# Products of the first four tiles of two modulation vectors on TensorE instead of VectorE

## The chip, the cores and the metric

The kernel runs on one core of a Trainium2 chip. The metric is device microseconds of that core for one execution; the time before is 2090.2 us, the median of 3 runs (2087.49 to 2090.66). Lower is better.

## The reference, cut to what matters

The model is two small transformer stacks, one after the other, on 256 tokens of width 1024. What the change touches is the very first step: the shift and the scale of the first normalisation, which are a matrix-vector product each.

```python
mod = (jax.nn.silu(c) @ ada_w[layer] + ada_b[layer]).reshape(B, 3, 3, D)
h = modulate_pre(x, g[0, 0], mod[:, 0, 0], mod[:, 0, 1])   # rms_norm(x, g) * (1 + scale) + shift
y = swiglu_ffn(h, ffn_w_in[layer, 0], ffn_w_out[layer, 0])
```

`c` is one row of 1024 numbers and each of shift and scale has 1024 entries, so either costs a read of a 1024 x 1024 float32 matrix (4 MB) that is used once.

## The kernel before, in words

All work is float32. Activations stand transposed, as 8 tiles `k` of 128 features x 256 tokens, and every large product is made of three products of rounded halves (`hi`, `lo`), marked fp32r in the trace. Weights come in pieces of 128 x 1024 float32 (512 KB) through one pool of six buffers, `raw`, each read by a transfer that SyncE (SP) issues as soon as a buffer is free; SP issues them in a fixed order.

`first_ffn` starts the program. It needs, for every tile `k`, two columns of 128 numbers: `b` (shift) and `a` (from the scale). Before the change both are made by VectorE (DVE): line 312 multiplies a 128 x 1024 piece of `ada_w`, laid out with outputs on partitions, by `srow`, a row silu(c) spread over all partitions, and sums along the row. Lines 315 to 317 add the bias and fold in the gain. A second chain makes the norm: `x` is loaded (line 267), turned by 16 TensorE (PE) transposes (line 274) that ScalarE (ACT) copies out (line 275), while ACT squares and sums `x` (line 395, four times), GpSimd (POOL) makes the reciprocal root of it (lines 402 to 404), PE spreads it over partitions (line 432) and ACT copies it out as `rb` (line 434). Only then can DVE make `tmp = xT * a * rb` (line 319), ACT `hi` (line 320) and DVE `lo` (line 321) of a tile.

A string sets how the eight tiles (A) and the first four weight blocks (W, each two pieces: line 300 on ACT, line 301 on DVE) follow each other in the program's text:

```python
 'start': 'AAAWAWAWAWAA',
```

`xk` is 2, so the pieces of tiles 0 and 1 are asked for ahead of `x`. `unit(s, k)` (lines 282 to 290) is the PE work of weight block `s` on tile `k`, six products of 128 x 256. A scheduler then orders each engine's instructions by its own forecast of times; the order on an engine is fixed from there on, and each engine takes its instructions in that order.

Of the kernel before, what the change touches and what calls it, by code (L numbers as in the profile page):

```python
# [13 lines left out]
F32 = mybir.dt.float32  # L14
BF16 = mybir.dt.bfloat16
F32R = mybir.dt.float32r
AF = mybir.ActivationFunctionType
ALU = mybir.AluOpType
# [3 lines left out]
P = 128  # L22
D = 1024
KT = D // P
# [61 lines left out]
class Kern:  # L86
# [176 lines left out]
    def first_ffn(self, g, win):  # L263
        nc, I = self.nc, self.I
        srow = self.srow(0)
        raws = [self.raw_half(I["ada_w"][v][k]) for k in range(self.cfg["xk"]) for v in range(2)]
        nc.sync.dma_start(self.x, I["x"])
        xT = self.chunk().rearrange("p (k t) -> p k t", k=KT)
        for q in range(4):
# [9 lines left out]
        ab = self.cp.tile([P, KT, 2], F32, name=self.name("AB"))  # L279
# [13 lines left out]
        for item in self.cfg["start"]:  # L293
            if item == "W":
                s = len(ws)
                whi, wlo = self.chunk(F32R), self.chunk(F32R)
                for half in range(2):
                    c = slice(half * 1024, (half + 1) * 1024)
                    raw = self.raw_half(win[s][:, c])
                    nc.scalar.copy(whi[:, c], raw)  # L300
                    nc.vector.tensor_tensor(wlo[:, c], raw, whi[:, c].bitcast(F32), op=ALU.subtract)
                ws.append([(whi[:, h * 1024:(h + 1) * 1024], wlo[:, h * 1024:(h + 1) * 1024]) for h in range(2)])
                pss.append([self.ps([P, T], "ps" if s < 3 else "fps") for _ in range(2)])
                for k in range(done):
                    unit(s, k)
                continue
            k = done
            a, b = ab[:, k, 1:2], ab[:, k, 0:1]
            for v in range(2):
                raw = raws[2 * k + v] if 2 * k < len(raws) else self.raw_half(I["ada_w"][v][k])  # L310
                junk = self.w([P, D], "vjunk", bufs=1, dt=BF16)
                nc.vector.scalar_tensor_tensor(junk, raw, 1.0, srow, op0=ALU.mult, op1=ALU.mult,
                                               accum_out=ab[:, k, v:v + 1])
            bb, ba = (self.col("ada_b", v * 8 + k, 1) for v in range(2))
            nc.vector.tensor_tensor(b, b, bb, op=ALU.add)
            nc.vector.tensor_scalar(a, a, ba, 1.0, op0=ALU.add, op1=ALU.add)
            nc.vector.tensor_tensor(a, a, g[:, k:k + 1], op=ALU.mult)
            tmp = self.w([P, T], "htmp", bufs=2)
            nc.vector.scalar_tensor_tensor(tmp, xT[:, k], a, rb, op0=ALU.mult, op1=ALU.mult)
            nc.scalar.activation(hi[:, k], tmp, AF.Identity, bias=b)  # L320
            nc.vector.scalar_tensor_tensor(lo[:, k], tmp, b, hi[:, k].bitcast(F32), op0=ALU.add, op1=ALU.subtract)
            done += 1
            for s in range(len(ws)):
                unit(s, k)
# [1132 lines left out]
def host_layout(a):  # L1457
    f = lambda z: np.ascontiguousarray(z)
# [16 lines left out]
    def vecs(w):  # L1475
        return w.reshape(D, -1, KT, P).transpose(1, 2, 3, 0)
# [5 lines left out]
    o = {}  # L1482
# [2 lines left out]
    o["crow"] = f(np.stack([a["c"].reshape(D), a["c_2"].reshape(D), a["c_ctx_2"].reshape(D)]))  # L1485
    o["ctx"] = toks(a["ctx_2"])
    o["ada_w"] = f(np.concatenate([vecs(a["ada_w"][l]) for l in range(2)]))
    o["kv_ada_w"] = f(vecs(a["kv_ada_w"]))
    o["ada_w2"] = f(np.concatenate([vecs(a["ada_w_2"][l]) for l in range(2)]))
    o["ffn_w_in"] = f(np.concatenate([ffin(a["ffn_w_in"][l, i]) for l in range(2) for i in range(2)] + [ffin(a["ffn_w_gu_2"][l]) for l in range(2)]))  # L1490
# [75 lines left out]
```

## Time and profile before

| what | value |
|---|---|
| runs, median (range) | 2090.2 us (2087.49 to 2090.66) |
| the profiled execution | 2091.53 us, its span 2089.8 us |
| busy share of the span: PE, DVE, ACT, POOL | 95%, 78%, 52%, 7% |
| PE busy in the first of 40 slices (0 to 52 us), and in the next ones | 5 tenths; 9 tenths or more |
| chain that ended last: PE, DVE | 68%, 14% of the span |

The span runs from the first to the last instruction; the execution's own time is 1.7 us longer. The page gives the mean over the whole program. The change works in the first 50 us, so what is read below is the trace of that stretch.

### The profile page before, as it was taken

What the parts mean: (1) busy time and instruction counts of PE and PEld (TensorE: products, weight loads), DVE (VectorE), ACT (ScalarE), POOL (GpSimd) and SP (SyncE); (2) the same over time, 40 slices, a digit from 0 to 9 for tenths busy, and PEclk for the clock granted to TensorE, in tenths of its full rate; (3) what the DMA queues carried; (4) which work ended last, traced back from release to release, by engine and by line L of the source; (5) the groups of instructions that cost most, each with busy time, mean ns of one, the idle gap of its engine ahead of it and who ended that gap; (6) DMA issues with size and microseconds to landing.
All of it is one profiled execution on the core that took longest, in us unless ns stands there. A gap on an engine that the chain in (4) does not pass through costs nothing.

```text
span 2089.8 us, 34683 instructions
## 1 busy us (share of the span) xinstructions
PE 1995.1 (95%) x13158; PEld 1783.2 (85%) x13158; DVE 1625.2 (78%) x2753; ACT 1094.3 (52%) x1775; POOL 138.6 (7%) x188
## 2 busy tenths in 40 slices
PE   5999999999999999999999999999999999999998
PEld 5998797999889878888778999878888999778997
DVE  7878898877887788789988666889879855866454
ACT  3444545444554466657655444548755444564443
POOL 0000202000100000120001000210010000100000
PEclk9999999999999999999999999999999999999999
DMA  9999787899877775576457767565456955514553
GB/s 331 326 320 341 253 321 279 323 321 316 280 243 258 255 231 181 186 255 209 166 169 251 268 232 237 190 207 190 162 176 233 348 191 193 165 61 160 185 188 114
DMA packets 136327, 486.46 MB, mean 233 GB/s; under 512 B 14976, under 2 KB 16480, under 8 KB 135392
## 3 DMA queue, kind: packets, MB, share of 16 engines
q1 hardware_dynamic: 134240, 477.90, 66.9%
q0 software_dynamic: 1728, 6.29, 0.9%
q8 instruction: 103, 1.69, 0.3%
q14 instruction: 64, 0.52, 0.1%
q10 hardware_dynamic: 192, 0.05, 0.0%
HBM read 480.47 MB, written 3.19 MB: 231 GB/s over the span
## 4 chain that ended last, share of the span: by engine, by line
PE 68%; DVE 14%; ACT 5%; DMA 5%; issue 4%; POOL 3%; SPq 0%; DVEq 0%; POOLq 0%; ACTq 0%
DMA x<-in_x 0%; DVE x L641 0%; DVE xc L649 0%; DMA raw.kv.1194_6453<-in_kv_v 0%; PE ps.a10.1298_7028 L744 0%; ACT chunk.a11.1957_10411 L870 0%; DMA raw.a11.1891_10022<-in_ada_w 0%; PE ps.a10.1253_6706 L744 0%; ACT chunk.ctx.1429_7781 L1050 0%; DMA raw.a10.1424_7749<-in_ada_w 0%; DMA raw.a12.2451_13229<-in_ada_w 0%; DMA raw.a10.1455_7896<-in_ada_w 0%; POOL rqx L387 0%; DMA raw.bffn0.3229_17294<-in_ffn_w_in 0%; DMA raw.bffn0.3136_16851<-in_ada_w 0%
## 5 line engine op out<-in xcount | busy, mean ns | idle before, releaser
L1050 ACT ACT_TABLE_LOAD x16 | 20.5, 1283 | 1.7 <-DVE dst.diff0.2922_15807 L1048 1.4
L341 ACT ACT_TABLE_LOAD x16 | 20.5, 1283 | 0.3
L274 PE MATMUL ps.a00.6_101<-ident,x 128*128 128x128 f32 x4 | 1.1, 428 | 13.9 <-DMA x<-in_x 13.9
L274 PEld LDWEIGHTS ps.a00.6_101<-ident,x 128*128 128x128 f32 x4 | 0.7, 217 | 13.9 <-issue 13.9
L376 POOL DMA_DIRECT2D G.a12.2544_13849<-row.a12.2543_13847 x1 | 0.6, 595 | 179.5 <-DMA row.a12.2543_13847<-diag.a12.2542_13845 179.5
L376 POOL DMA_DIRECT2D G.bffn2.3890_21467<-row.bffn2.3889_21465 x1 | 0.6, 595 | 172.0 <-DMA row.bffn2.3889_21465<-diag.bffn2.3888_21463 172.0
L376 POOL DMA_DIRECT2D G.a02.1038_5659<-row.a02.1037_5657 x1 | 0.6, 612 | 166.1 <-DMA row.a02.1037_5657<-diag.a02.1036_5655 166.1
L334 ACT ACT_TABLE_LOAD x9 | 11.5, 1283 | 0.2
L376 POOL DMA_DIRECT2D G.bffn0.3422_18599<-row.bffn0.3421_18597 x1 | 0.6, 595 | 164.5 <-DMA row.bffn0.3421_18597<-diag.bffn0.3420_18595 164.5
L402 POOL TENSOR_TENSOR rv.ctx.354_2048<-ss.ctx.352_2044,epsd 128x1 f32<-128x1 f32 x1 | 0.2, 189 | 169.8 <-ACT junk.ctx.351_2043 L395 169.8
L376 POOL DMA_DIRECT2D G.a11.2178_11711<-row.a11.2177_11709 x1 | 0.6, 595 | 156.5 <-DMA row.a11.2177_11709<-diag.a11.2176_11707 156.5
L734 ACT ACTIVATE chunk.a10.1248_6656<-chunk.kv.1130_6083,cols 128x60 f32<-128x60 f32 x32 | 10.3, 385 | 0.8 <-ACT chunk.kv.1220_6568 L461 0.8
L288 PE MATMUL ps.a00.38_198<-chunk.a00.20_148,chunk.a00.34_188 128*128 128x256 f32 x8 | 3.2, 405 | 5.4 <-ACT chunk.a00.34_188 L300 2.9
L485 ACT CAST chunk.a01.490_2583<-chunk.a01.492_2585 128x256 fp32r<-128x256 f32 x8 | 3.2, 406 | 9.1 <-DVE chunk.a01.492_2585 L677 9.1
L288 PEld LDWEIGHTS ps.a00.38_198<-chunk.a00.20_148,chunk.a00.34_188 128*128 128x128 f32 x8 | 1.9, 236 | 6.4 <-ACT chunk.a00.20_148 L320 3.2
L387 POOL TENSOR_TENSOR rqc<-rv.ctx.1311_7159,nhalf 128x8 f32<-128x8 f32 x1 | 1.6, 1647 | 80.5 <-DVE rv.ctx.1311_7159 L383 80.5
L870 ACT ACT_TABLE_LOAD x5 | 6.4, 1283 | 0.1
L976 DVE TENSOR_TENSOR chunk.diff0.2633_14301<-chunk.diff0.2633_14301,chunk.diff0.2632_14300 128x512 f32<-128x512 f32 x8 | 5.5, 687 | 0.0
L493 PE MATMUL fps.ctx.2170_11637<-chunk.ctx.1879_9995,whi.ctx.2163_11623 128*128 128x256 f32 x8 | 3.1, 390 | 2.4 <-DVE xc L649 2.4
L349 ACT ACTIVATE srow<-srow 128x1024 f32<-128x1024 f32 x3 | 3.2, 1059 | 4.1 <-DMA srow<-in_crow 4.1
L177 DVE SCALAR_TENSOR_TENSOR vjunk.a12.2497_13512<-raw.a12.2477_13400,srow 128x1024 bf16<-128x1024 f32 x1 | 1.2, 1227 | 5.3 <-DMA raw.a12.2477_13400<-in_ada_w 5.3
L376 POOL DMA_DIRECT2D G.a01.634_3484<-row.a01.633_3482 x1 | 0.6, 617 | 69.0 <-DMA row.a01.633_3482<-diag.a01.632_3480 69.0
(11976 smaller groups left out, 9411.7 us busy)
## 6 DMA issues: line engine op xcount, KB each, us to landing
srow<-in_crow SPq DMA_DIRECT2D x3, 512.0 KB
x<-in_x SPq DMA_DIRECT2D x1, 1024.0 KB
xc<-in_ctx SPq DMA_DIRECT2D x1, 1024.0 KB
kvd<-chunk.ctx.451_2428 SPq DMA_DIRECT2D x1, 1024.0 KB, 9.8
kvd<-chunk.ctx.452_2429 SPq DMA_DIRECT2D x1, 1024.0 KB
chunk.diff0.2772_15017<-kvd SPq DMA_DIRECT2D x1, 1024.0 KB, 8.0
chunk.diff0.2773_15018<-kvd SPq DMA_DIRECT2D x1, 1024.0 KB
out<-x SPq DMA_DIRECT2D x2, 512.0 KB
```

What stands on the lines that cost most here:

```text
L274: nc.tensor.transpose(ps[:, k, t * P:(t + 1) * P], self.x[:, t, kt * P:(kt + 1) * P], self.ident)
L288: mm(out, whi[:, ks], hi[:, k], start=(k == 0), stop=False)
L334: nc.scalar.activation(sg, gate, AF.Silu)
L341: nc.scalar.activation(sg, gate, AF.Silu)
L349: self.nc.scalar.activation(t, t, AF.Silu)
L376: nc.gpsimd.dma_start(G, src.to_broadcast([P, D]))
L485: nc.scalar.copy(hi, src)
L493: mm(out, shi, mhi, start=first, stop=False)
L734: nc.scalar.activation(bt[:, j], self.kv2[i][:, :, 2 * j:2 * j + 16 * (NCMP - 1) + 1:16], AF.Identity, bias=self.col("pos", 16 * i + j, 1))
L870: nc.scalar.activation(p[:, br], p[:, br], AF.Exp, bias=mx[:, par, br:br + 1], accum_out=sm[:, br, par:par + 1])
L976: nc.vector.tensor_tensor(o, o, o2, op=ALU.add)
L1050: nc.scalar.activation(e[:, :nk], ps[:, :nk], AF.Exp, bias=st[:, m:m + 1], scale=r, accum_out=st[:, 2 + m:3 + m])
```

## The change

The weights of tiles 0 to 3 of both vectors get a second copy, `ada_w0`, with the 1024 inputs on partitions: piece `[v][k]` is 128 x 1024, eight blocks `d` of 128 inputs x 128 outputs. silu(c) is made a second time as a 128 x 8 array `scol` (one ACT instruction). For these tiles the DVE product falls away; instead PE runs eight products, each with a 128 x 128 float32 block of the piece as the weights and one column of `scol` as the moving operand, summed in one column of a PSUM tile `vps`. DVE then reads bias sums from that tile. Tiles 4 to 7 stay as they were.

```diff
-        raws = [self.raw_half(I["ada_w"][v][k]) for k in range(self.cfg["xk"]) for v in range(2)]
+        npe = I["ada_w0"].shape[1]
+        first = lambda v, k: I["ada_w0"][v][k] if k < npe else I["ada_w"][v][k]
+        raws = [self.raw_half(first(v, k)) for k in range(self.cfg["xk"]) for v in range(2)]
+        sc = self.cp.tile([P, KT], F32, name="scol")
+        nc.scalar.activation(sc, self.col("c"), AF.Silu)
+        vps = self.ps([P, 2 * npe], "fps")
...
-                raw = raws[2 * k + v] if 2 * k < len(raws) else self.raw_half(I["ada_w"][v][k])
+                raw = raws[2 * k + v] if 2 * k < len(raws) else self.raw_half(first(v, k))
+                if k < npe:
+                    for d in range(KT):
+                        nc.tensor.matmul(vps[:, 2 * k + v:2 * k + v + 1], raw[:, d * P:(d + 1) * P], sc[:, d:d + 1],
+                                         start=(d == 0), stop=(d == KT - 1))
+                    continue
                 junk = self.w([P, D], "vjunk", bufs=1, dt=BF16)
...
-            nc.vector.tensor_tensor(b, b, bb, op=ALU.add)
-            nc.vector.tensor_scalar(a, a, ba, 1.0, op0=ALU.add, op1=ALU.add)
+            bs, as_ = (vps[:, 2 * k + v:2 * k + v + 1] if k < npe else ab[:, k, v:v + 1] for v in range(2))
+            nc.vector.tensor_tensor(b, bs, bb, op=ALU.add)
+            nc.vector.tensor_scalar(a, as_, ba, 1.0, op0=ALU.add, op1=ALU.add)
...
+    o["ada_w0"] = f(a["ada_w"][0][:, :2 * D].reshape(KT, P, 2, KT, P).transpose(2, 3, 1, 0, 4)
+                    [:, :4].reshape(2, 4, P, D))
```

Lines of the changed kernel are 5 to 13 further down: 279 is the transpose of line 274, 280 the copy of line 275, 293 to 295 are lines 288 to 290, 326 to 328 lines 315 to 317, 406 is line 395, 443 line 432, 445 line 434.

PE, from its first instruction to the spreading of the norm, after the change (`raw` 1 to 4 are the pieces of tiles 0 and 1, `raw` 26 and 27 those of tile 2, each row eight one-column products unless it says otherwise):

```order
L318 MATMUL fps.a00.5_101<-scol,raw.a00.1_91 128x1 x8
L318 MATMUL fps.a00.5_101<-scol,raw.a00.2_93 128x1 x8
L318 MATMUL fps.a00.5_101<-scol,raw.a00.3_95 128x1 x8
L318 MATMUL fps.a00.5_101<-scol,raw.a00.4_97 128x1 x8
L279 MATMUL ps.a00.7_104<-ident,x 128x128 x4
L279 MATMUL ps.a00.8_110<-ident,x 128x128 x4
L279 MATMUL ps.a00.9_116<-ident,x 128x128 x4
L279 MATMUL ps.a00.10_122<-ident,x 128x128 x4
L318 MATMUL fps.a00.5_101<-scol,raw.a00.26_200 128x1 x8
L318 MATMUL fps.a00.5_101<-scol,raw.a00.27_210 128x1 x8
L443 MATMUL ps.a00.19_146<-ident,rr.a00.13_132 128x128
L443 MATMUL ps.a00.19_146<-ident,rr.a00.17_141 128x128
```

Before the change the 16 transposes are PE's first work and the two products of the norm stand right behind them; now 32 one-column products stand ahead of the transposes and 16 more between them and the norm. The first product of tile 1 also waits for DVE, which reads tile 0's two columns of `vps` first; so does tile 2's.

PE, from the first unit of the first weight block (`raw` 35 and 36 are the pieces of tile 3):

```order
L293 MATMUL ps.a00.33_237<-chunk.a00.21_151,chunk.a00.29_227 128x256
L294 MATMUL ps.a00.33_237<-chunk.a00.22_152,chunk.a00.29_227 128x256
L318 MATMUL fps.a00.5_101<-scol,raw.a00.35_257 128x1 x8
L293 MATMUL ps.a00.34_238<-chunk.a00.21_151,chunk.a00.29_227 128x256
L294 MATMUL ps.a00.34_238<-chunk.a00.22_152,chunk.a00.29_227 128x256
```

Tile 3's products stand among the units of the first weight block: two products of 128 x 256 ahead of the first eight, and seven (these two are the first of them) between the first eight and the eight of `raw` 36.

ACT, from the first sum of squares of `x` to `rb`, before the change:

```order
L395 ACTIVATE junk.a00.10_125,ss.a00.11_126<-x 128x512 x2
L275 COPY chunk.a00.5_100<-ps.a00.6_101 128x512
L395 ACTIVATE junk.a00.14_134,ss.a00.15_135<-x 128x512
L275 COPY chunk.a00.5_100<-ps.a00.7_107 128x512
L395 ACTIVATE junk.a00.14_134,ss.a00.15_135<-x 128x512
L275 COPY chunk.a00.5_100<-ps.a00.8_113 128x512
L275 COPY chunk.a00.5_100<-ps.a00.9_119 128x512
L434 ACTIVATE rb.a00.19_146<-ps.a00.18_143 128x256
```

and after it:

```order
L270 ACTIVATE scol<-cols 128x8
L406 ACTIVATE junk.a00.11_128,ss.a00.12_129<-x 128x512
L280 COPY chunk.a00.6_103<-ps.a00.7_104 128x512
L280 COPY chunk.a00.6_103<-ps.a00.8_110 128x512
L280 COPY chunk.a00.6_103<-ps.a00.9_116 128x512
L280 COPY chunk.a00.6_103<-ps.a00.10_122 128x512
L406 ACTIVATE junk.a00.11_128,ss.a00.12_129<-x 128x512
L406 ACTIVATE junk.a00.15_137,ss.a00.16_138<-x 128x512 x2
L445 ACTIVATE rb.a00.20_149<-ps.a00.19_146 128x256
```

Three of the four sums of squares now stand behind all four copies, which wait for the transposes; before, two of the four stood ahead of the first copy and the others between copies.

On DVE the eight instructions of line 312 for tiles 0 to 3 are gone. Tile 3's small sums (line 326) now stand ahead of the second weight block's two differences (line 306), which before stood on either side of them. SP and POOL keep their order. Behind the first 60 us no engine's order changes.

## Rows read from the trace of the kernel before

**Rows 1.** Busy time of the engines by stage; the first two numbers are stretch and length.

```profile
core 0: us, PE busy (x) PEld busy (x) DVE busy (x) ACT busy (x) POOL busy (x), PEclk, DMA share, GB/s
...
25.48:48.50 23.02, 18.86 (x136) 17.44 (x135) 22.74 (x46) 6.45 (x10) 0.00 (x0) 1.00 0.95 332
60.00:195.00 135.00, 135.00 (x958) 127.48 (x957) 108.41 (x147) 62.09 (x75) 2.89 (x6) 1.00 0.92 329
```

**Rows 2.** Timeline, DVE: start us, us; in brackets the idle time before and what ended it.

```profile
7.54 1.23 DVE L312 SCALAR_TENSOR_TENSOR vjunk.a00.23_151<-raw.a00.1_91,srow 128x1024 bf16<-128x1024 f32 x1 [1.22 <-DMA raw.a00.1_91<-in_ada_w]
...
20.41 0.48 DVE L319 SCALAR_TENSOR_TENSOR htmp.a00.25_158<-chunk.a00.5_100,AB.a00.22_150,rb.a00.19_146 128x256 f32<-128x256 f32 x1 [2.34 <-ACT rb.a00.19_146 L434]
```

**Rows 3.** Timeline, the chain of the norm over ACT, POOL and PE.

```profile
13.79 0.63 ACT L395 ACTIVATE junk.a00.10_125<-x 128x512 bf16<-128x512 f32 x1 [7.40 <-DMA x<-in_x]
...
14.54 0.63 ACT L395 ACTIVATE junk.a00.10_125<-x 128x512 bf16<-128x512 f32 x1
...
17.82 0.60 ACT L275 COPY chunk.a00.5_100<-ps.a00.9_119 128x512 f32<-128x512 f32 x1
...
18.02 0.18 POOL L402 TENSOR_TENSOR rv.a00.17_139<-ss.a00.15_135,epsd 128x1 f32<-128x1 f32 x1
...
19.16 0.80 PE L432 MATMUL ps.a00.18_143<-ident,rr.a00.16_138 128*128 128x128 f32 x2 [0.26 <-POOL rr.a00.16_138 L404]
```

**Rows 4.** Timeline, PE: the transposes of x, second and fourth group of four.

```profile
14.78 1.06 PE L274 MATMUL ps.a00.7_107<-ident,x 128*128 128x128 f32 x4
...
16.48 1.06 PE L274 MATMUL ps.a00.9_119<-ident,x 128*128 128x128 f32 x4
```

**Rows 5.** Timeline, PE: the same 128 x 256 products ahead of a wait and behind it.

```profile
23.20 0.42 PE L289 MATMUL ps.a00.38_198<-chunk.a00.21_149,chunk.a00.34_188 128*128 128x256 f32 x1
...
25.43 0.41 PE L290 MATMUL ps.a00.39_199<-chunk.a00.20_148,chunk.a00.35_189 128*128 128x256 f32 x1
25.64 0.41 PE L288 MATMUL ps.a00.39_199<-chunk.a00.20_148,chunk.a00.34_188 128*128 128x256 f32 x1
...
29.23 0.39 PE L290 MATMUL ps.a00.49_249<-chunk.a00.20_148,chunk.a00.46_240 128*128 128x256 f32 x1 [1.25 <-DVE chunk.a00.46_240 L301]
...
30.05 0.28 PE L288 MATMUL ps.a00.49_249<-chunk.a00.20_148,chunk.a00.45_239 128*128 128x256 f32 x1
30.17 0.28 PE L289 MATMUL ps.a00.49_249<-chunk.a00.21_149,chunk.a00.45_239 128*128 128x256 f32 x1
```

**Rows 6.** Timeline, PE: float32 products of few columns, lines 764 and 744.

```profile
632.03 0.90 PE L764 MATMUL ps.a10.1262_6807<-htmp.a10.1261_6805,chunk.kv.1129_6080 128*64 128x15 f32 x16
632.86 0.39 PE L493 MATMUL ps.a10.1264_6827<-chunk.kv.1220_6568,whi.a10.1267_6831 128*128 128x256 f32 x1
...
651.04 1.06 PE L744 MATMUL ps.a10.1298_7028<-chunk.a10.1248_6656,raw.a10.1285_6975 128*128 128x60 f32 x8
...
656.40 1.06 PE L744 MATMUL ps.a10.1298_7028<-chunk.a10.1248_6656,raw.a10.1287_6979 128*128 128x60 f32 x8
```

**Rows 7.** Line 432 alone: ns min/median/max of one, first and last start.

```profile
L432 PEld LDWEIGHTS ps.a00.18_143<-ident,rr.a00.12_129 x2: 288/313/338, 18.1 to 18.3; 128*128 128x128 f32 x2
L432 PE MATMUL ps.a00.18_143<-ident,rr.a00.12_129 x2: 422/500/579, 18.1 to 18.5; 128*128 128x128 f32 x2
...
L432 PEld LDWEIGHTS ps.a00.474_2516<-ident,rr.a00.431_2361 x2: 188/188/188, 238.8 to 239.1; 128*128 128x128 f32 x2
```

**Rows 8.** Timeline, DVE: tiles 3 and 4.

```profile
25.48 1.22 DVE L312 SCALAR_TENSOR_TENSOR vjunk.a00.41_220<-raw.a00.40_218,srow 128x1024 bf16<-128x1024 f32 x1
...
30.95 1.22 DVE L312 SCALAR_TENSOR_TENSOR vjunk.a00.52_277<-raw.a00.51_275,srow 128x1024 bf16<-128x1024 f32 x1
...
33.64 0.16 DVE L315 TENSOR_TENSOR AB.a00.22_150<-AB.a00.22_150,cols 128x1 f32<-128x1 f32 x1
...
34.60 1.22 DVE L301 TENSOR_TENSOR chunk.a00.57_303<-raw.a00.58_304,chunk.a00.56_302 128x1024 fp32r<-128x1024 f32 x1
35.73 0.48 DVE L321 SCALAR_TENSOR_TENSOR chunk.a00.21_149<-htmp.a00.55_286,AB.a00.22_150,chunk.a00.20_148 128x256 fp32r<-128x256 f32 x1
```

## The prediction, made before the changed kernel ran

> **What bounds the kernel now.** I read the table of stages first, for the place where an engine that the change touches is the limit. From 25.48 to 48.50 us VectorE is busy 22.74 of 23.02 us while TensorE waits about 4.2 us; from 60 us on TensorE is busy for the whole of 135.00 us [rows 1]. So the program's first 50 us are a run of VectorE work that feeds TensorE, and afterwards TensorE is the limit. Everything after 50 us stands in a fixed order behind this start, so a shift of the start by so many microseconds moves the end by as many.
>
> Then I read VectorE's timeline. Its first product begins at 7.54 us, when its piece lands, and products of tiles 0 to 2 run until it has to wait 2.34 us for `rb`, which ends at 20.41 us [rows 2]. I call that moment T0: from there VectorE hardly stops. The six products of tiles 0 to 2 therefore lie in time that VectorE has to spare; taking them away gives nothing. Only tile 3's two products, from 25.48 us on, lie on the path.
>
> The third view is the chain that ends in `rb`: `x` lands at 13.79 us, the squares and the transposes follow, ScalarE's last copy starts at 17.82 and is 0.60 long, GpSimd's last step begins at 18.02, and the second spreading product starts at 19.16 us, 1.25 us ahead of T0 [rows 2, 3]. This chain, not the modulation vectors, sets T0 before the change. The change puts new work on both TensorE and ScalarE in front of it.
>
> **The price of the new products.** One piece costs eight products. A true float32 product runs as two records, each with its own weight load (the one product of line 432 shows two of each [rows 7]), so a piece is 16 records of 128 columns of weights and one moving column. The trace has no such record at one column. Three rows bound it.
>
> The transposes, 128 moving columns, follow each other at (16.48 - 14.78) / 8 = 0.2125 us [rows 4]. That is at the lower of the clock's two levels, 1.2 GHz: 128 x 256 products are 0.21 us apart at 25.43 and 0.12 us at 30.05, and the step comes behind the wait that ends at 29.23, after TensorE had done nothing but wide products since 22.8 us [rows 5]. The clock column reads 1.00 in these stages; I go by the pitch. The 16 transposes in a row did not lift the clock.
>
> At the higher level, 2.4 GHz, 60 moving columns follow each other at (656.40 - 651.04) / 48 = 0.112 us; with half as many weight columns and 15 moving columns the pitch is (632.86 - 632.03) / 16 = 0.052 us [rows 6]. So the weight load sets the pitch, 128 columns in 0.11 us, and fewer moving columns save nothing: 16 x 0.112 = 1.79 us a piece at the higher level.
>
> At the lower level a first weight load of line 432 takes 288 ns against 188 at the higher one [rows 7]. The 100 ns more is what a load of 0.11 us gains when it doubles, so I take 0.2125 us here too: 16 x 0.2125 = 3.40 us a piece. VectorE's product of the same piece takes 1.23 us [rows 2]. Bounds: 0.83 us (the 0.052 pitch) and 3.40 us. I take 3.40, since one-column products ask even less of the array than transposes do, and those left the clock low.
>
> The Trainium skill, TensorE: Matmul & The Clock Gate, LDWEIGHTS (loading the stationary operand), gives a load of 128 columns as 107 ns and names no clock level; the row at the higher level agrees with 0.112, and no row at the lower level is limited by loads alone. By the page a piece would cost 1.71 us throughout, which is close to the second rival below.
>
> **The change, step by step, at 3.40 us a piece.** TensorE starts at 7.54 us, as VectorE did. Tile 0 takes 6.8 us. Tile 1 waits for VectorE to read tile 0's columns: 0.42 us until a product is out [rows 7] and two small instructions, 0.8 us in all as an estimate. Tile 1 6.8, the 16 transposes 3.4, tile 2 6.8, the first spreading product 0.43, and 1.25 from the second to T0:
>
> 7.54 + 6.8 + 0.8 + 6.8 + 3.4 + 6.8 + 0.43 + 1.25 = 33.8 us, **13.4 us later** than 20.41.
>
> ScalarE's new order is hidden by this: the transposes end at 25.3; before, the last copy ended 1.1 us behind the last transpose, so now at 26.4; three sums of squares at 14.54 - 13.79 = 0.75 us and POOL's last 1.14 us [rows 3] come to 29.8, ahead of TensorE's 32.5. Without that cover it would cost 2.7 us (below). `scol` runs while ScalarE waits for `x`.
>
> Behind T0, tile 3. The second wide product starts at 23.20 [rows 5], T0 + 2.8, and is through 0.21 later. Then piece one, seven wide products (7 x 0.2125 = 1.5), piece two, and 0.5 to hand over: T0 + 3.0 + 3.4 + 1.5 + 3.4 + 0.5 = T0 + 11.8. Before, VectorE went on at 25.48 = T0 + 5.07. It now waits 6.7 us there, with the second weight block's two differences queued behind (they stood ahead or between before). From there to tile 4's first product: 0.55 for three small sums, about 0.4 each for lines 319 and 321, and twice 34.60 to 35.73 = 1.13 for the differences, 3.6 in all: T0 + 15.4 against 30.95 = T0 + 10.54. Tile 4's two products end with one 0.4 us instruction fewer between them [rows 8]: **4.5 us later**, the 2.5 us of tile 3's removed products already counted in.
>
> The rest of the run to 50 us is unchanged VectorE work; TensorE has some 4 us of waits there to take up its late units. Reads: those of the first weight block now wait until TensorE, not VectorE, is through with a piece (from about 11 us), but they land long before T0; reads for tile 4 go out when tile 3's pieces are released, five or more microseconds ahead of need. SP's and POOL's orders stay.
>
> Sum: 13.4 + 4.5 = 17.9 us. The profiled execution took 2091.5 us (its span 2089.8), so it would be 2109.4; it lies 1.3 us above the median of the runs, and against that median I predict **2108 us**. 0.2%, 4.2 us, is about what a measurement can tell from no change.
>
> **The rivals.**
> *The clock rises.* If the one-column products are work enough, TensorE is at the higher level after tile 0. Tiles 1 and 2 then take 3.58 us each, the transposes 1.7; they end at 7.54 + 6.8 + 0.8 + 3.58 + 1.7 = 20.4, ScalarE and POOL need 1.1 + 2.25 + 1.14 more, and T0 = 24.9 + 1.25 = 26.1, 5.7 late. Tile 3 is ready at T0 + 7.6, which leaves +0.3: **2096 us**. The Trainium skill's same page, Part 1: The HAM clock gate, says that sustained work releases the lower level; by that rule this rival holds if such products count, and rows 5 show a rise only behind wide ones.
> *Loads don't slow with the clock.* At the higher level's 0.112 us a load also at the lower one, 1.79 us a piece: transposes end at 7.54 + 3.58 + 0.8 + 3.58 + 3.4 = 18.9, T0 = 18.9 + 4.5 + 1.25 = 24.6, +4.2; tile 3 is ready at T0 + 8.6, +1.3: **2096 us** as well. Against it stands the first load's 288 ns.
> *Not slower.* If a one-column record is much cheaper than any row shows, the transposes start with `x` at 13.9 and end at 17.3, but the three sums of squares behind the copies still give T0 = 17.3 + 4.5 + 1.25 = 23.1, 2.7 late. At 0.83 us a piece tile 3 comes at T0 + 6.7, 0.6 ahead of before in effect: +2.1, **2092 us**; at nothing, 2.2 ahead: +0.5. It decides at 0.097 us a record (1.55 a piece), below which the result is within 0.2%. For less than nothing I see no mechanism but the drift of the clock's later drops, a microsecond or two.
>
> **How the numbers follow.** Low clock throughout 0.55; clock rises 0.2; loads at a fixed rate 0.13; cheap records 0.12. The first alone spans 2102 (pitch 0.165, the distance of line 432's two loads, 18.1 to 18.3: 11.9 us) to 2111. The range reaches down to the cheap case at 2092. Slower by over 0.2% means above 2094.4: all of the first and most of the two middle cases, 0.78; within 0.18; faster 0.04.
>
> **What would show it.** In the changed trace: 16 records a piece at about 0.21 us from 7.5 us on; transposes of `x` starting near 22 us instead of 13.9; the wait for `rb` ending near 34 us; a VectorE wait of six or seven microseconds for `fps` behind it; and from 60 us on the same TensorE rows, all later by the same amount. The prediction is wrong if the pitch is 0.11 us or less, if the clock rises within the first products, or if the shift at 60 us is not the shift at the end.

## The result, and the profile after

The changed kernel takes 2107.07 us (median of 4 runs, 2104.55 to 2111.95) against 2090.43 us (4 runs, 2087.49 to 2093.40) for the kernel before: a recorded ratio of 1.0094, with a 95% interval of 1.0079 to 1.0110; the quotient of the two medians, 1.0080, lies at the lower end of it. By the medians it is slower by 16.6 us, under one per cent; 2108 was predicted. The profiled execution took 2107.18 us, its span 2105.4, which is 15.6 longer than the span before.

The first view is TensorE's timeline of the changed kernel (start, length, engine, line; x16 is the number of records).

```profile
7.56 3.54 PE L318 MATMUL fps.a00.5_101<-scol,raw.a00.1_91 128*128 128x1 f32 x16 [7.56 <-DMA raw.a00.1_91<-in_ada_w]
10.97 3.55 PE L318 MATMUL fps.a00.5_101<-scol,raw.a00.2_93 128*128 128x1 f32 x16
14.90 3.58 PE L318 MATMUL fps.a00.5_101<-scol,raw.a00.3_95 128*128 128x1 f32 x16 [0.38 <-DVE AB.a00.23_153 L327]
...
21.75 1.09 PE L279 MATMUL ps.a00.7_104<-ident,x 128*128 128x128 f32 x4
...
32.45 0.64 PE L443 MATMUL ps.a00.19_146<-ident,rr.a00.17_141 128*128 128x128 f32 x2
35.95 0.58 PE L293 MATMUL ps.a00.33_237<-chunk.a00.21_151,chunk.a00.29_227 128*128 128x256 f32 x1 [2.87 <-ACT chunk.a00.29_227 L305]
36.33 0.42 PE L294 MATMUL ps.a00.33_237<-chunk.a00.22_152,chunk.a00.29_227 128*128 128x256 f32 x1
36.55 3.41 PE L318 MATMUL fps.a00.5_101<-scol,raw.a00.35_257 128*128 128x1 f32 x16
...
41.45 3.41 PE L318 MATMUL fps.a00.5_101<-scol,raw.a00.36_267 128*128 128x1 f32 x16
44.72 0.56 PE L295 MATMUL ps.a00.34_238<-chunk.a00.21_151,chunk.a00.30_228 128*128 128x256 f32 x1
```

Sixteen records take 10.97 - 7.56 = 3.41 us, 0.213 us each. Four pieces stand ahead of the first transpose, which starts at 21.75 us in place of 13.90, and two more ahead of the spreading products. The first transposes before the change:

```profile
13.90 1.09 PE L274 MATMUL ps.a00.6_101<-ident,x 128*128 128x128 f32 x4 [13.90 <-DMA x<-in_x]
```

The second view is VectorE's timeline of the changed kernel.

```profile
32.06 0.16 DVE L326 TENSOR_TENSOR AB.a00.23_153<-fps.a00.5_101,cols 128x1 f32<-128x1 f32 x1 [9.65 <-PE fps.a00.5_101 L318]
...
33.53 0.48 DVE L330 SCALAR_TENSOR_TENSOR htmp.a00.24_173<-chunk.a00.6_103,AB.a00.23_153,rb.a00.20_149 128x256 f32<-128x256 f32 x1 [1.00 <-ACT rb.a00.20_149 L445]
...
44.90 0.16 DVE L326 TENSOR_TENSOR AB.a00.23_153<-fps.a00.5_101,cols 128x1 f32<-128x1 f32 x1 [6.21 <-PE fps.a00.5_101 L318]
...
48.55 1.22 DVE L322 SCALAR_TENSOR_TENSOR vjunk.a00.45_328<-raw.a00.44_326,srow 128x1024 bf16<-128x1024 f32 x1
```

T0, the start of the first line 330 (line 319 before, 20.41 in [rows 2]), is at 33.53 us. Behind it stands the predicted wait for `fps`, 6.21 us, and tile 4's first product starts at 48.55 us against 30.95 in [rows 8]. The table of waits, over the first 75 us, puts a price on it (total us, times, longest):

```profile
DVE AB.a00.23_153 L326 <- PE fps.a00.5_101 L318: 31.0, 4, 9.7
```

Most of these 31 us are time that VectorE had to spare, since its products of the four tiles are gone. What counts is how late the start ends. I take the `lo` of tile 7, the last small step of the start on VectorE, as its end. Before and after it reads:

```profile
51.37 0.48 DVE L321 SCALAR_TENSOR_TENSOR chunk.a00.21_149<-htmp.a00.82_475,AB.a00.22_150,chunk.a00.20_148 128x256 fp32r<-128x256 f32 x1
```

```profile
68.70 0.48 DVE L332 SCALAR_TENSOR_TENSOR chunk.a00.22_152<-htmp.a00.75_526,AB.a00.23_153,chunk.a00.21_151 128x256 fp32r<-128x256 f32 x1
```

It is 17.33 us later. From there to the end of the span it is 2089.8 - 51.37 = 2038.4 us before and 2105.4 - 68.70 = 2036.7 after, so 1.7 us came back on the way. They came back in one place: VectorE's instructions still stand 17.3 us later around 200 us (line 177 at 199.37 before and 216.70 after) and again at 1000 us, with 17.0 to 18.5 in between, but 15.5 at 1040. From 990 to 1020 us the kernel before was granted 0.66, 0.91 and 0.92 of the clock in three stretches of 10 us, the changed one 0.83, 1.00 and 1.00 in the same stretches 17 us on. In all thirteen traces of this study the remainder lies between 2032.6 and 2041.2 us. The kernel before alone varies by more: its 29 runs beside the last experiments lie between 2080.62 and 2094.39 us. (The four latest starts have the remainders 2032.6 to 2036.7, the other nine 2032.8 to 2041.2; whether some of a late start comes back is not shown.) I judge the experiments by the end of the start, which is free of this, and give the measured time beside it. It is one trace for each kernel, and moves by a few tenths with the landing of the first piece (7.19 to 7.69 us).

### The profile page after: what moved, and what is told of

Its sections match the earlier page's. It is cut to its first block, busy times and chain, and to the rows that moved or that the text cites. A ratio compares the mean times of both kernels' runs of the same rounds, so it can differ in the third digit from the quotient of the medians.

```text
span 2105.4 us, 34925 instructions
## 1 busy us (share of the span) xinstructions
PE 2021.1 (96%) x13286; PEld 1811.7 (86%) x13286; DVE 1615.5 (77%) x2737; ACT 1095.0 (52%) x1776; POOL 136.7 (6%) x188
## 4 chain that ended last, share of the span: by engine, by line
PE 64%; DVE 16%; DMA 7%; issue 5%; ACT 5%; POOL 3%; DVEq 0%; SPq 0%; POOLq 0%; ACTq 0%
PE fps.a00.5_101 L318 1%; DVE xc L660 0%; DVE x L652 0%; ACT chunk.ctx.1422_7832 L1061 0%; DMA raw.a10.1312_7231<-in_ffn_w_in 0%; ACT chunk.a11.1950_10462 L881 0%; DMA raw.a11.1884_10073<-in_ada_w 0%; PE ps.a10.1246_6757 L755 0%; DMA raw.ctx.1372_7532<-in_ada_w 0%; DMA raw.bffn0.3283_17660<-in_ffn_w_in 0%; DMA raw.a10.1417_7800<-in_ada_w 0%; DMA raw.a01.544_2984<-in_a_w_in 0%; DMA raw.a12.2444_13280<-in_ada_w 0%; DMA raw.bffn0.3236_17424<-in_ffn_w_out 0%; DMA raw.bffn0.3129_16902<-in_ada_w 0%
## 5 line engine op out<-in xcount | busy, mean ns | idle before, releaser
L745 ACT ACTIVATE chunk.a10.1241_6707<-chunk.kv.1123_6134,cols 128x60 f32<-128x60 f32 x32 | 10.4, 387 | 0.8 <-ACT chunk.kv.1213_6619 L472 0.8
```

Source lines behind the costliest of these rows:

```text
L745: nc.scalar.activation(bt[:, j], self.kv2[i][:, :, 2 * j:2 * j + 16 * (NCMP - 1) + 1:16], AF.Identity, bias=self.col("pos", 16 * i + j, 1))
```

## The experiments

The theory: eight pieces at 3.41 us each, set by the loading of 128 weight columns at the lower clock, fill TensorE's queue, and everything behind the start is late by that. The rivals: (A) the lateness of T0, because pieces stand ahead of the norm's chain, is the cost; (B) each piece costs alike wherever it stands; (C) ScalarE's new order or the hand-over through `fps`; (D) a fixed cost of a record. The next table has what was measured; in each row the ratio is to the kernel before in runs beside it on the same chip. The medians of those runs differ, so medians of different rows can't be compared as they stand: 2088.20 us beside tile 3, tile 0, one block and half the weight columns; 2086.74 beside four blocks, norm first, wide products and 64 columns; 2087.24 beside the last three.

| kernel | T0, us | end of start, us (to before) | median, us | ratio, 95% interval |
|---|---|---|---|---|
| before | 20.41 | 51.37 | 2090.43 | |
| changed | 33.53 | 68.70 (+17.3) | 2107.07 | 1.0094, 1.0079 to 1.0110 |
| tile 3 only | 20.17 | 57.24 (+5.9) | 2097.03 | 1.0041, 1.0027 to 1.0055 |
| tile 0 only | 22.12 | 53.08 (+1.7) | 2091.54 | 1.0012, 0.9998 to 1.0027 |
| one block of eight | 22.21 | 51.49 (+0.1) | 2088.56 | 1.0005, 0.9988 to 1.0021 |
| four blocks of eight | 23.63 | 55.36 (+4.0) | 2097.17 | 1.0050, 1.0034 to 1.0065 |
| half the weight columns | 23.68 | 56.11 (+4.7) | 2093.48 | 1.0029, 1.0016 to 1.0041 |
| norm first | 19.83 | 69.92 (+18.6) | 2105.72 | 1.0098, 1.0077 to 1.0119 |
| wide products ahead | 31.04 | 66.19 (+14.8) | 2100.59 | 1.0074, 1.0047 to 1.0102 |
| 64 moving columns | 29.78 | 66.02 (+14.7) | 2101.08 (one run) | |
| 128 moving columns | 22.90 | 53.27 (+1.9) | 2092.03 | 1.0027, 1.0012 to 1.0042 |
| before, four tiles first | 21.15 | 50.55 (-0.8) | 2087.83 | 1.0006, 0.9993 to 1.0019 |
| the same, sums on VectorE | 19.38 | 48.78 (-2.6) | 2088.35 | 1.0005, 0.9989 to 1.0020 |

### Which tiles cost: tile 3 alone, tile 0 alone

```diff
+        pes = (3,)
...
-                if k < npe:
+                if k in pes:
...
```

> Only tile 3's two products run on TensorE; tiles 0 to 2 are on VectorE as before the change. Main theory (weight loads of 0.213 us a record, 3.41 us a piece, in TensorE's queue): T0 back at about 20.4 us, since nothing stands ahead of the transposes; behind T0 the two pieces and some 16 wide products of 0.21 us lie on TensorE, so tile 3 is ready about 13 us behind T0 in place of 7.5, and everything after is some 5.5 us later than before the change: about 2096 us. Rival A (the cost is all ahead of the norm chain, tile 3's own move is paid by the 2.5 us that VectorE saves): within 1 us of before, 2090 to 2091. Rival B (every piece costs the same wherever it stands, 17 us / 8 = 2.1 us each): 2095, which this run can't tell from the main theory by the time alone, but then T0 would be late.

T0 is where it was, and the start ends 5.9 us later. This rules out (A) for this part: with the norm's chain undisturbed, tile 3's two pieces cost 5.9 us by themselves. VectorE's timeline of this kernel shows the wait:

```profile
33.45 0.16 DVE L327 TENSOR_TENSOR AB.a00.23_153<-fps.a00.5_101,cols 128x1 f32<-128x1 f32 x1 [8.13 <-PE fps.a00.5_101 L319]
```

Tile 3 is ready 13.3 us behind T0, as worked out (13). The second piece is cut in two here by nine wide products, so the wait is longer than the 6.21 us of the changed kernel. The same edit with `pes = (0,)`:

> Only tile 0's two products run on TensorE. Main theory: 7.5 + 2 x 3.41 = 14.4 us, 0.5 us behind the moment at which the transposes could begin (13.9), so T0 is at most 0.6 us later and the program the same as before the change, 2090 to 2091.5 us. Rival B (every piece costs about 2.1 us wherever it stands): 2094.5. Rival C (the move of work on ScalarE that the scheduler makes is what costs): as before too, since the order of ScalarE's squares and copies here is that of before.

The start ends 1.7 us later, not 0.6 at most: under half of what (B) says, but more than the theory. Two pieces cost 5.9 us at tile 3 and 1.7 at tile 0, so (B) is out by the traces; the time with tile 0 (1.0012, 0.9998 to 1.0027) can't tell. The transposes start at 14.37 as expected. What is late is GpSimd; its timeline of this kernel:

```profile
17.93 1.23 POOL L414 TENSOR_TENSOR rv.a00.18_142<-ss.a00.16_138,epsd 128x1 f32<-128x1 f32 x1
19.23 1.26 POOL L415 TENSOR_TENSOR rv.a00.18_142<-rv.a00.18_142,ss.a00.16_138 128x1 f32<-128x1 f32 x1
20.57 0.55 POOL L416 TENSOR_TENSOR rr.a00.17_141<-rv.a00.18_142,nhalf 128x1 f32<-128x1 f32 x1
```

and VectorE's beside it:

```profile
17.89 1.22 DVE L323 SCALAR_TENSOR_TENSOR vjunk.a00.29_190<-raw.a00.28_188,srow 128x1024 bf16<-128x1024 f32 x1
...
19.23 1.22 DVE L323 SCALAR_TENSOR_TENSOR vjunk.a00.31_194<-raw.a00.30_192,srow 128x1024 bf16<-128x1024 f32 x1
```

The first of them, line 402 before the change, took 0.18 us in [rows 3], on one number a partition. Here the first two of the three steps end as VectorE's products end. Tile 0's wait for TensorE pushed VectorE's products of tiles 1 and 2 back until they lay over GpSimd's steps. The last two experiments come back to this.

### What sets the price of a piece

One block only (seven eighths of the sum are left out), and four blocks (half of the sum is left out); `1` and `0` in place of `4` and `3` for the first:

```diff
-                    for d in range(KT):
+                    for d in range(4):
...
-                                         start=(d == 0), stop=(d == KT - 1))
+                                         start=(d == 0), stop=(d == 3))
```

> All four tiles on TensorE but one product of eight for each piece, which leaves out seven eighths of the sum. ScalarE keeps the changed order (squares behind all four copies), and VectorE waits for the column as in the changed kernel. Main theory: 0.43 us a piece, 0.85 us a tile, so the transposes start with x at 13.9 us; T0 is late by the ScalarE order alone, 2.7 us; behind T0 tile 3 costs nothing, and VectorE saves 2.5 us: between 2089.5 and 2092 us. Rival C (the order on ScalarE, or the hand-over through the fps buffer, is the larger part of the cost): 2100 us or more.

> The changed kernel with four of a piece's eight products (half of the sum is left out): 8 records a piece in place of 16, each as wide as before. Main theory, and every theory in which the cost goes by records: 1.7 us a piece, transposes near 15.1 us, T0 near 24.3, tile 3 ready at T0 + 8.4, about 5 us over before: 2095 us. It is the yardstick for the run with half the weight columns. If the time falls by less than half of the 17 us (2100 or more), something besides the records costs.

Half the weight columns, which leaves out half of the outputs of the four tiles:

```diff
+        nc.vector.memset(vps, 0.0)
...
-                        nc.tensor.matmul(vps[:, 2 * k + v:2 * k + v + 1], raw[:, d * P:(d + 1) * P], sc[:, d:d + 1],
+                        nc.tensor.matmul(vps[0:64, 2 * k + v:2 * k + v + 1], raw[:, d * P:d * P + 64], sc[:, d:d + 1],
```

> All products stay, 16 records a piece, but each loads 64 columns of weights in place of 128 (half of each vector is left out). Main theory (the columns of the load set the pitch): 0.107 us a record, 1.7 us a piece; transposes start near 15.1 us, T0 near 24.3, tile 3 ready at T0 + 8.4: about 5 us over before, 2095 us. Rival D (a fixed cost of a record or of its issue, whatever its width): pitch stays 0.213 and the time stays 2107. Rival E (part fixed, part by columns, 0.06 + 64 x 0.0012 = 0.14 us): 2098 to 2100.

TensorE's timeline with half the weight columns, and with four blocks:

```profile
7.46 1.84 PE L319 MATMUL fps.a00.5_101<-scol,raw.a00.1_91 128*64 128x1 f32 x16 [7.46 <-DMA raw.a00.1_91<-in_ada_w]
9.16 1.84 PE L319 MATMUL fps.a00.5_101<-scol,raw.a00.2_93 128*64 128x1 f32 x16
```

```profile
7.69 1.84 PE L318 MATMUL fps.a00.5_101<-scol,raw.a00.1_91 128*128 128x1 f32 x8 [7.69 <-DMA raw.a00.1_91<-in_ada_w]
9.39 1.84 PE L318 MATMUL fps.a00.5_101<-scol,raw.a00.2_93 128*128 128x1 f32 x8
```

Sixteen loads of 64 columns and eight of 128 take the same 1.70 us: 0.106 and 0.213 us a record, in proportion to the columns loaded. That rules out (D), and the part-fixed cost of rival E. By the start both give back about three quarters of the 17.3 us for half of the loading, since the transposes then start at 14.89 and 15.05 us, about 1 us late. By the time only half the weight columns agrees (5.3 us over before beside it). Four blocks are 10.4 us over, with an interval of 7.1 to 13.6, for a start only 4.0 us later; that is less than half of 16.6 given back. In its trace VectorE still stands 4.0 us later at 200 us and 3.7 at the end, so the rest does not lie in the start; where it lies stays open. With one block the start ends 0.1 us late although ScalarE's order and the hand-over are those of the changed kernel; T0 is 1.8 us late there, and VectorE's missing products make up for it. That rules out (C) as the larger part of the cost. It is also close to the prediction's third rival at its limit (+0.5 us for records that cost nothing).

### Amount or place: the norm first

Tiles 1 to 3 take their moving column from a copy that waits for the norm.

```diff
-        rb = self.bcast([self.norm_r(self.x, t) for t in range(TT)], "ps")
+        rr = [self.norm_r(self.x, t) for t in range(TT)]
+        rb = self.bcast(rr, "ps")
+        zero = self.cp.tile([P, 1], F32, name="zero")
+        nc.gpsimd.tensor_scalar(zero, rr[1], 0.0, None, op0=ALU.mult)
+        sc2 = self.cp.tile([P, KT], F32, name="scol2")
+        nc.scalar.activation(sc2, self.col("c"), AF.Silu, bias=zero)
...
-                        nc.tensor.matmul(vps[:, 2 * k + v:2 * k + v + 1], raw[:, d * P:(d + 1) * P], sc[:, d:d + 1],
+                        nc.tensor.matmul(vps[:, 2 * k + v:2 * k + v + 1], raw[:, d * P:(d + 1) * P], (sc2 if k else sc)[:, d:d + 1],
```

> The changed kernel, but tiles 1 to 3 take their moving column from a second copy that is made behind the norm, so that the transposes and the spreading products stand ahead of tile 1 on TensorE; the amount of work is the same. T0 would be near 21 us. Main theory (TensorE's sum of work up to tile 3 is the bound: eight pieces of 3.41, transposes 3.4 and the first wide products): tile 3 is ready near 44 to 46 us as in the changed kernel, and the time stays at 2105 to 2110 us although T0 is 12 us earlier. Rival A (the delay of T0 is the cost, as the 13.4 us in the prediction's sum reads): some 9 to 12 us come back, 2095 to 2098 us.

T0 is at 19.83 us, earlier than before the change, and nothing comes back. VectorE's timeline has its waits for tiles 1, 2 and 3 instead:

```profile
25.00 0.16 DVE L331 TENSOR_TENSOR AB.a00.23_157<-fps.a00.5_101,cols 128x1 f32<-128x1 f32 x1 [4.68 <-PE fps.a00.5_101 L323]
...
32.36 0.16 DVE L331 TENSOR_TENSOR AB.a00.23_157<-fps.a00.5_101,cols 128x1 f32<-128x1 f32 x1 [5.97 <-PE fps.a00.5_101 L323]
...
44.99 0.16 DVE L331 TENSOR_TENSOR AB.a00.23_157<-fps.a00.5_101,cols 128x1 f32<-128x1 f32 x1 [8.56 <-PE fps.a00.5_101 L323]
```

Tile 3 is ready at 44.99 us, against 44.90 in the changed kernel, and the start ends 1.2 us later still. So the delay of T0 is not the cause. The cause is TensorE's sum of work up to tile 3, and the order only decides who waits for it first. That the two moments agree to 0.1 us is partly luck: here tile 1's pieces gained 2.0 us from a higher clock (below), and nine more products of 128 x 256, 1.9 us, stand ahead of tile 3's pieces.

### The clock: wide products ahead, 64 and 128 moving columns

First 15 wide products on zeros in TensorE's idle time ahead of the first piece:

```diff
+        wt = self.w([P, D], "vjunk", bufs=1, dt=BF16)
+        nc.vector.memset(wt, 0.0)
+        wps = self.ps([P, 512], "fps")
+        for _ in range(15):
+            nc.tensor.matmul(wps, wt[:, 0:P], wt[:, 0:512], start=True, stop=True)
```

> The changed kernel with 15 wide products (bfloat16, 512 moving columns, on zeros, read by nobody) in TensorE's idle time ahead of 7.5 us. At the lower clock they take 0.43 us each, 6.4 us in all, some 1.2 to 7.9 us. If the clock rises behind them and the one-column products hold it: pitch 0.112, 1.79 us a piece, transposes near 16, T0 near 24, tile 3 ready at T0 + 8: 2092 to 2096 us. If the one-column products don't count as work that holds it: the pitch falls back to 0.213 within the first pieces, and the time stays within 3 us of 2107. If the clock does not rise at all: 2107 to 2108.

TensorE's timeline, and behind it the busy times by stretch (the figure behind POOL's is the granted clock, as a share of 2.4 GHz):

```profile
1.52 5.98 PE L276 MATMUL fps.a00.7_104<-vjunk.a00.6_102 128*128 128x512 bf16 x15 [1.52 <-DVE vjunk.a00.6_102 L273]
7.50 1.92 PE L323 MATMUL fps.a00.5_101<-scol,raw.a00.1_91 128*128 128x1 f32 x16
9.28 2.74 PE L323 MATMUL fps.a00.5_101<-scol,raw.a00.2_93 128*128 128x1 f32 x16
12.40 3.58 PE L323 MATMUL fps.a00.5_101<-scol,raw.a00.3_95 128*128 128x1 f32 x16 [0.38 <-DVE AB.a00.25_171 L332]
```

```profile
7.50:11.00 3.50, 3.50 (x29) 3.50 (x29) 0.00 (x0) 0.00 (x0) 0.00 (x0) 0.88 1.04 430
11.00:19.00 8.00, 7.62 (x36) 7.54 (x37) 0.45 (x3) 0.72 (x2) 0.19 (x1) 0.50 0.99 398
```

The wide products lifted the clock, and the first piece ran at (9.28 - 7.50) / 16 = 0.111 us a record. Then, with TensorE busy in 3.50 of 3.50 us on records of one column, the clock fell to 0.50, 1.2 GHz, and the pieces went back to 0.213 us. This is the second of the three cases that were written down by its mechanism. Its time there, within 3 us of 2107, was missed as it stands (2100.59) and met against the kernel before beside it, 13.9 us over where the changed kernel is 16.6. It also settles the prediction's rival in which loads don't slow with the clock: the same load takes 0.111 us at one level and 0.213 at the other.

The level also rose, and fell again, without wide products ahead. TensorE's timeline with the norm first, behind the transposes and the spreading products:

```profile
20.04 1.95 PE L323 MATMUL fps.a00.5_101<-scol,raw.a00.3_95 128*128 128x1 f32 x16 [0.66 <-ACT scol L286]
21.85 3.11 PE L323 MATMUL fps.a00.5_101<-scol,raw.a00.4_97 128*128 128x1 f32 x16
25.34 3.58 PE L323 MATMUL fps.a00.5_101<-scol,raw.a00.26_204 128*128 128x1 f32 x16 [0.38 <-DVE AB.a00.23_157 L332]
```

The first piece takes 21.85 - 20.04 = 1.81 us, 0.113 us a record; the level is lost within the second, and the third is at 0.214 again. With four blocks the first piece behind the transposes takes 0.81 us in place of 1.70, too. So in these two traces the level rose at or behind the transposes, where in the kernel before and in the changed one it did not. What decides that is not shown.

Then one column, spread to 64 equal ones by ScalarE:

```diff
...
-                        nc.tensor.matmul(vps[:, 2 * k + v:2 * k + v + 1], raw[:, d * P:(d + 1) * P], sc[:, d:d + 1],
+                        nc.tensor.matmul(vps[:, 2 * k + v], raw[:, d * P:(d + 1) * P], scw[:, d],
...
```

> The changed kernel with 64 equal moving columns in place of one for each of the new products; the rest as it was. Main theory (the load of 128 weight columns sets the pitch): 0.213 us a record still and about the same time, 2105 to 2110 us. If moving columns add to the load: 64 more at 1.2 GHz are 0.053 us, pitch 0.266, 4.3 us a piece, about 2113 us. If more moving columns are what lifts the clock: the pitch falls to 0.112 within the first tiles, 2095 us.

TensorE's timeline, and the busy times of a later stretch:

```profile
7.57 3.65 PE L320 MATMUL fps.a00.5_101<-vjunk.a00.6_102,raw.a00.1_91 128*128 128x64 f32 x16 [7.57 <-DMA raw.a00.1_91<-in_ada_w]
11.01 3.62 PE L320 MATMUL fps.a00.5_101<-vjunk.a00.6_102,raw.a00.2_93 128*128 128x64 f32 x16
...
24.42 0.60 PE L281 MATMUL ps.a00.11_124<-ident,x 128*128 128x128 f32 x4
24.86 1.90 PE L320 MATMUL fps.a00.5_101<-vjunk.a00.6_102,raw.a00.27_202 128*128 128x64 f32 x16
```

```profile
32.00:42.00 10.00, 9.81 (x49) 9.81 (x49) 2.88 (x4) 3.38 (x5) 0.00 (x0) 0.53 0.47 159
```

The first two pieces start at 7.57 and 11.01 us: 0.215 us a record, so 64 moving columns cost next to nothing. The clock rose 24 us in, among the transposes, and was granted at 0.53 again from 32 to 42 us. Since it rose there with one column too (norm first, four blocks), this run does not show that the 64 columns lifted it; and TensorE had waited 2.87 us ahead of 32.19 us, so it does not show that they failed to hold it. The result is between the cases written down, 2.7 us gained at the end of the start. Last, 128 columns, by reading one column 128 times:

```diff
-        vps = self.ps([P, 2 * npe], "fps")
+        vps = self.ps([P, 2 * npe + 128], "fps")
...
-                        nc.tensor.matmul(vps[:, 2 * k + v:2 * k + v + 1], raw[:, d * P:(d + 1) * P], sc[:, d:d + 1],
+                        nc.tensor.matmul(vps[:, 2 * k + v:2 * k + v + 128], raw[:, d * P:(d + 1) * P],
+                                         sc[:, d:d + 1].to_broadcast([P, 128]),
...
```

> The changed kernel with 128 equal moving columns (a column read 128 times) in place of one. With 64 the records stayed at 0.213 us and the clock rose among the transposes, 24 us in, and fell again; tile 4's first product stood at 45.9 us against 48.6. If it is the moving columns that the clock answers to and the load alone sets the pitch: 0.213 us at first, the rise within the first two tiles and no fall behind it, 1.8 us a piece from there, tile 4's first product at 36 to 40 us, time 2095 to 2099. If the clock answers only to wide products of the other kind: pitch 0.213 throughout and 2104 to 2108 us. If 128 moving columns no longer hide behind the load: pitch over 0.25 us, 2110 us or more.

TensorE's timeline:

```profile
7.29 3.75 PE L318 MATMUL fps.a00.5_101<-scol,raw.a00.1_91 128*128 128x128 f32 x16 [7.29 <-DMA raw.a00.1_91<-in_ada_w]
10.84 2.80 PE L318 MATMUL fps.a00.5_101<-scol,raw.a00.2_93 128*128 128x128 f32 x16
14.02 2.05 PE L318 MATMUL fps.a00.5_101<-scol,raw.a00.3_95 128*128 128x128 f32 x16 [0.38 <-DVE AB.a00.23_153 L328]
...
16.13 0.60 PE L279 MATMUL ps.a00.7_104<-ident,x 128*128 128x128 f32 x4
...
26.91 0.28 PE L293 MATMUL ps.a00.33_237<-chunk.a00.21_151,chunk.a00.29_227 128*128 128x256 f32 x1
27.03 0.28 PE L294 MATMUL ps.a00.33_237<-chunk.a00.22_152,chunk.a00.29_227 128*128 128x256 f32 x1
```

The first piece takes 3.55 us (0.222 a record), the clock rises within the second, and the third takes 15.90 - 14.02 = 1.88 us. It does not fall again among the pieces: at 26.91 us the wide products stand 0.12 us apart, the higher level's pitch in [rows 5]. Tile 4's first product starts at 32.41 us, 3.6 us ahead of the window that was written down, since the transposes and the wide products gain from the clock too. Only when TensorE had waited 2.53 us ahead of 35.99 us did the level fall (0.63 from 36 to 38 us). Doing 128 times the arithmetic, with the same loads, gives back 15.4 of the 17.3 us, and the ratio falls from 1.0094 to 1.0027.

TensorE's order is not quite that of the changed kernel here: the transposes stand ahead of most of tile 1's second piece, and the spreading products ahead of most of tile 2's records. So the 1.9 us left are not the price of the loads alone. For the changed kernel's order and a clock that rises behind tile 0 the prediction worked out 5.7 + 0.3 = 6.0 us; as an estimate from the two, the lower clock is 11 to 15 of the 17.3 us, most of the cost of the change. The order at the higher clock was not run apart. By the time 4.8 us are left (2092.03 against 2087.24), with an interval of 2.5 to 8.8.

### A version without TensorE products

If VectorE has 2.34 us to spare ahead of `rb` [rows 2], tile 3's products could go there. First the order alone, in the kernel before:

```diff
- 'start': 'AAAWAWAWAWAA',
+ 'start': 'AAAAWAWAWAWA',
```

> The kernel before with one number changed, the order at the start: tile 3's two products stand ahead of the first weight block, so that VectorE does them in the 2.34 us in which it waits for rb. No product goes to TensorE. If they fit into that wait at no cost: everything behind is some 2.4 us earlier, 2086 to 2088 against 2088 to 2090 for before. Rival F (GpSimd's three short steps on the norm stand still while VectorE runs a long product, as the run with tile 0 alone showed: 1.23 and 1.26 us in place of 0.18 and 0.19): T0 is 1 to 2 us late and the gain behind it is 0.5 to 1.5 us at most, which the time can't tell from none; the position of tile 4's first product tells it (30.95 before).

Then the sums of the norm on VectorE, for the start only:

```diff
...
-        g = self.nc.gpsimd
+        g = self.nc.vector if self.dve_norm else self.nc.gpsimd
...
+        if self.dve_norm:
+            g.tensor_scalar(v, ss[:, 0:1], ss[:, 1:2], D * EPS, op0=ALU.add, op1=ALU.add)
+            self.nc.gpsimd.tensor_tensor(r, v, self.nhalf[:, 0:1], op=ALU.pow)
+            return r
```

> As the run before it, and the two sums of each norm step go to VectorE as one instruction, so that GpSimd has one step for each half in place of three. If GpSimd standing still behind VectorE's products is what holds T0 (rival F): T0 is 1 us or more earlier than in the run before it, and tile 4's first product 1 us earlier too. If the chain is set by ScalarE's squares: no difference between the two. Time for both readings 2085 to 2089 us.

GpSimd's timeline with the order alone:

```profile
17.71 1.23 POOL L402 TENSOR_TENSOR rv.a00.17_139<-ss.a00.15_135,epsd 128x1 f32<-128x1 f32 x1
```

It starts with VectorE's first product of tile 3 (17.68 us) and ends with it; T0 is at 21.15. With the sums on VectorE T0 is at 19.38, and the end of the start goes from 0.8 to 2.6 us ahead of before:

```profile
19.38 0.48 DVE L322 SCALAR_TENSOR_TENSOR htmp.a00.25_156<-chunk.a00.5_100,AB.a00.22_148,rb.a00.19_144 128x256 f32<-128x256 f32 x1 [0.17 <-ACT rb.a00.19_144 L441]
```

In the trace that is the step that held T0 (rival F). In the time neither can be told from the kernel before: 1.0006 (0.9993 to 1.0019) and 1.0005 (0.9989 to 1.0020). 2.6 us is less than the remainder of the program wanders, so no version here is shown to be faster than the kernel before.

## Why the prediction was right

**The price.** 3.40 us a piece was taken, 3.41 came. That it is set by the columns of the load, and not by the moving column or the record, was argued from [rows 4, 6 and 7]; the runs with half the weight columns and with 64 moving columns show it.

**The clock.** That one-column products would leave it at the lower level was an inference from the transposes, with a chance of 0.2 for a rise. In the changed kernel it was low for all eight pieces, and where it was high they let it fall (wide products ahead, norm first). The step from the transposes to this was weaker than it reads, and there was luck in it: with the norm first and with four blocks the level did rise at or behind those same transposes. The prediction weighed a rule of the Trainium skill against its choice (TensorE: Matmul & The Clock Gate, Part 1: The HAM clock gate), that sustained work releases the lower level. It did not hold for the one-column pieces of the changed kernel; it held when they were made 128 columns wide. The result then was 4.8 us over the kernel before beside it, where the rival's 2096 is 5.8 over, but with T0 2.5 us late and not 5.7. By the Trainium skill's same page (section LDWEIGHTS) a load of 128 columns works out to 107 ns. That agrees with 0.111 us at the higher level; at the lower one it was 0.213.

**T0.** 33.8 us was predicted and 33.53 came. The hand-over from tile 0 to tile 1 took 0.52 us (10.97 + 3.41 to 14.90) in place of 0.8. ScalarE's order was hidden, as said: neither spreading product waits for GpSimd in the changed trace. One reading is off without weight in the sum: the step of GpSimd at 18.02 us [rows 3] is the first of its last three, and the 1.14 us are all three.

**Behind T0.** Tile 3 was ready at T0 + 11.37 (predicted 11.8) after a wait of 6.21 (6.7), and tile 4 started at T0 + 15.02 (15.4). The hand-over took 0.18 us (44.72 to 44.90) in place of 0.5, and a piece between wide products 3.26 (36.55 to 39.81) in place of 3.4.

**The sum.** 17.9 us was predicted and 17.33 stands at the end of the start; the span grew by 15.6 and the medians differ by 16.6. The prediction's last test, that the shift at 60 us be the shift at the end, held to 0.1 us around 200 us and failed by 1.7 us at the end; the place, with its different granted clock, is the drift of a microsecond or two that the prediction names.

**What it had wrong in reading.** The sum sets 13.4 us down to the norm's chain and 4.5 to tile 3. The number is right, the division is not a cause: with the norm first T0 is not late at all, and the start still ends 18.6 us late, behind waits for tiles 1, 2 and 3. Nor do the parts add: tile 3 alone costs 5.9 us, not 4.5. And the rival of cheap records drew its line of 4.2 us at 0.097 us a record. Four blocks come to 1.70 us a piece, as 0.106 us a record would; the prediction's terms make that 5.0 us, and the start ended 4.0 us late, tile 2's faster pieces included. So by the start the line lies a little higher than drawn, and by the time (10.4 us) lower. The rival itself is out: a record costs 0.213 us.

## What to carry to other kernels

The matrix-vector product on TensorE paid here for its weights, not for its arithmetic: count records, times the time to load their columns, at the clock that this stream itself will be granted. Where one moving column left the clock at its lower level, reading that column 128 times cost 0.222 us a record in place of 0.213 here, and the higher level came within the second piece. And when work is put in front of a chain, ask what is the sum on the engine up to the point that needs it all; taking it out from in front of the chain gives nothing if that sum is the bound.

## What the runs showed of the hardware that was not expected

- TensorE busy without a gap on one-column float32 records, each with a load of 128 columns, dropped from 2.4 to 1.2 GHz, from 0.111 to 0.213 us a record (within 9.28 to 12.02 us in the run with wide products ahead, within 21.85 to 24.96 with the norm first). With 128 moving columns the same loads went from 0.222 to 0.117 us a record (1.88 / 16) by the third piece, and the level stayed for all later pieces. That is one trace, but the ten runs of that kernel, 2085.31 to 2096.80 us, all lie under the fastest of the changed one, 2104.55.
- The clock column can't be taken at its word at the start. In the changed kernel's busy times, from 7.50 to 14.40 us, it reads 1.00, while the same records at the same 0.213 us stand under 0.50 in the run with wide products ahead; the pitch is the safer reading, and why the column differs stays open:

```profile
7.50:14.40 6.90, 6.84 (x32) 6.87 (x32) 0.00 (x0) 0.60 (x2) 0.00 (x0) 1.00 1.02 422
```

- A GpSimd step on 128 x 1 that takes 0.18 us alone takes 1.23 us when it starts beside a VectorE product of 128 x 1024, and ends when that ends; moving the two sums to VectorE brought T0 from 21.15 to 19.38 us. The Trainium skill (SBUF — State Buffer, section Who interferes with whom) describes the pair of ports that the two share as an exclusive lock; the rows agree with that. The kernel before pays for it as well: in the first half of its norm two steps lie beside tile 2's products (15.05 to 17.62 us) and take 0.92 and 1.63 us. That fits T0 coming 1.0 us earlier than before with the sums on VectorE. GpSimd's timeline before the change:

```profile
15.41 0.92 POOL L403 TENSOR_TENSOR rv.a00.13_130<-rv.a00.13_130,ss.a00.11_126 128x1 f32<-128x1 f32 x1 [0.62 <-ACT junk.a00.10_125 L395]
16.41 1.63 POOL L404 TENSOR_TENSOR rr.a00.12_129<-rv.a00.13_130,nhalf 128x1 f32<-128x1 f32 x1
```
